# 3-D instance norm: one-pass statistics on VectorE, all normalisation on ScalarE, six buffers with stores four tiles behind the loads

## The chip, the cores and the metric

The kernel runs on one core of a Trainium2 chip. The metric is the device time of one execution in microseconds (us). Before the change it is 1252.36 us, the median of 8 runs that lie between 1251.52 and 1253.71 us. The engines that matter are VectorE (DVE in the profile), ScalarE (ACT), GpSimd (POOL), TensorE (PE), and SyncE (SP), which issues the DMAs here. Sixteen DMA engines carry them out.

## What is computed

```python
def setup_inputs():
    batch, channels, (d, h, w) = 8, 64, (32, 64, 64)
    return {"x": np.random.randn(batch, channels, d, h, w).astype(np.float32), "eps": np.float32(1e-5)}

def reference(x, eps):
    mean = np.mean(x, axis=(2, 3, 4), keepdims=True)
    var = np.var(x, axis=(2, 3, 4), keepdims=True)
    return ((x - mean) / np.sqrt(var + eps)).astype(np.float32)
```

There are 8 x 64 = 512 instances of 32 x 64 x 64 = 131,072 float32 values. Each gets its own mean and variance. The input is 268.44 MB and so is the output. Every value is read once and written once.

## The kernel before

**Tiling.** Each instance is cut into 16 rows of 8,192 values, and 8 instances fill the 128 partitions of a tile (`SPLIT` = 16, `IPT` = 8, `F` = 8,192). That makes 64 tiles of 4,096 KB (4.19 million bytes). Group and tile are the same here, since `KPG` is 1. The buffers of the tiles come from a pool of four (line 45), 32 KB a partition each. A tile is normalised in place and stored from the same buffer.

**One tile.** `issue_load` (line 85) puts the load of one tile on the SP queue. `issue_compute` then does the following.

- VectorE sums each row in one instruction over 8,192 values (line 92). Beside it ScalarE squares the same values and accumulates their sum (line 100). The squares themselves go to a bfloat16 scratch tile that nobody reads.
- TensorE adds up the 16 rows of each instance with one small product (line 108). It multiplies by `ones_t`, a 128x128 block matrix that holds 1/16.
- VectorE and ScalarE work out mean, variance, `std`, `scale` and `bias` on operands of one or two values a partition (lines 117 to 149).
- Three engines normalise the tile: VectorE the first 1,024 columns, ScalarE the next 1,024, GpSimd the other 6,144 (lines 158 to 176, `norm_splits` at line 76).

**Order.** One loop goes over the 64 tiles. Its order on the SP queue is: load of tile g, then store of tile g - 2 (`LAG` = 2, lines 182 to 190). SP works its list off strictly in order. The first three loads go out at once, then the store of tile 0, the load of tile 3, the store of tile 1, and so on by turns. After the loop the last two stores follow. Two kinds of wait stand in this list. A store waits until all three engines have normalised their share of its tile. A load waits until the store that last used its buffer, four tiles back, has landed completely. The scheduler puts in these waits; the order itself is that of the Python loop.

**DMA.** A transfer covers 128 rows of 32,768 bytes. The trace shows each row as one packet, so a transfer has 128 packets, 8 for each of the 16 DMA engines. Each engine reports the end of its own share, so each transfer has sixteen landing events in the trace, and it counts as landed with the last of them. All loads and stores run on one DMA queue, named q1 in the profile. Two more kinds of record, on q14 and q8 with the kind `instruction`, belong to no line of the kernel.

Of the kernel before, what the change touches and what calls it, by code (L numbers as in the profile page):

```python
# [1 line left out]

# [4 lines left out]


@with_exitstack
def kernel(  # L10
    ctx: ExitStack,
    tc: tile.TileContext,
    x: bass.AP,
    eps: bass.AP,
    out: bass.AP,
):
    nc = tc.nc
    fp32 = mybir.dt.float32

    P = 128  # L20
    B, C, D, H, W = x.shape
    n_inst = B * C
    n_elem = D * H * W

    eps_f = float(eps)

    SPLIT = 16
    IPT = P // SPLIT
    F = n_elem // SPLIT

    G = 8
    KPG = G // IPT
    n_groups = n_inst // G

    LAG = 2

    x_packed = x.rearrange("b c d h w -> (b c) (d h w)").rearrange(
        "(k i) (s f) -> k (i s) f", i=IPT, s=SPLIT
    )
    out_packed = out.rearrange("b c d h w -> (b c) (d h w)").rearrange(  # L40
        "(k i) (s f) -> k (i s) f", i=IPT, s=SPLIT
    )

    singles = ctx.enter_context(tc.tile_pool(name="singles", bufs=1))
    data_pool = ctx.enter_context(tc.tile_pool(name="data", bufs=4))
    scratch_pool = ctx.enter_context(tc.tile_pool(name="scratch", bufs=2))
    stat_pool = ctx.enter_context(tc.tile_pool(name="stats", bufs=4))
    psum_pool = ctx.enter_context(tc.tile_pool(name="psum", bufs=4, space=bass.MemoryType.PSUM))

    ones_t = singles.tile([P, P], fp32)  # L50
    nc.vector.memset(ones_t, 1.0 / SPLIT)  # L51
    blk_pattern = [[-SPLIT, P // SPLIT], [0, SPLIT]]
    nc.gpsimd.affine_select(  # L53
        out=ones_t,
        in_=ones_t,
        pattern=blk_pattern,
        compare_op=mybir.AluOpType.is_ge,
        fill=0.0,
        base=0,
        channel_multiplier=1,  # L60
    )
    nc.gpsimd.affine_select(  # L62
        out=ones_t,
        in_=ones_t,
        pattern=[[SPLIT, P // SPLIT], [0, SPLIT]],
        compare_op=mybir.AluOpType.is_ge,
        fill=0.0,
        base=SPLIT - 1,
        channel_multiplier=-1,
    )  # L70

    inv_F = 1.0 / F

    c1 = F // 8
    c2 = F // 4
    norm_splits = [
        (nc.vector, 0, c1),
        (nc.scalar, c1, c2),
        (nc.gpsimd, c2, F),
    ]  # L80

    def issue_load(g):
        x_tiles = data_pool.tile([P, KPG, F], fp32, name="x_tiles")
        src = x_packed[g * KPG : (g + 1) * KPG].rearrange("k p f -> p k f")
        nc.sync.dma_start(out=x_tiles, in_=src)
        return x_tiles

    def issue_compute(g, x_tiles):
        psums = stat_pool.tile([P, KPG, 2], fp32, name="psums")

        for k in range(KPG):
            nc.vector.reduce_sum(  # L92
                out=psums[:, k, 0:1],
                in_=x_tiles[:, k, :],
                axis=mybir.AxisListType.X,
            )
            sq_scratch = scratch_pool.tile(
                [P, F], mybir.dt.bfloat16, name="sq_scratch"
            )
            nc.scalar.activation(  # L100
                out=sq_scratch,
                in_=x_tiles[:, k, :],
                func=mybir.ActivationFunctionType.Square,
                accum_out=psums[:, k, 1:2],
            )

        tot = psum_pool.tile([P, KPG, 2], fp32, name="tot")
        nc.tensor.matmul(  # L108
            out=tot,
            lhsT=ones_t,  # L110
            rhs=psums,
            start=True,
            stop=True,
        )

        me2 = stat_pool.tile([P, KPG, 2], fp32, name="me2")
        nc.vector.tensor_scalar(  # L117
            out=me2,
            in0=tot,
            scalar1=inv_F,  # L120
            scalar2=None,
            op0=mybir.AluOpType.mult,
        )
        mean = me2[:, :, 0]
        e2 = me2[:, :, 1]

        msq = stat_pool.tile([P, KPG], fp32, name="msq")
        nc.vector.tensor_mul(out=msq, in0=mean, in1=mean)  # L128

        var_eps = stat_pool.tile([P, KPG], fp32, name="var_eps")  # L130
        nc.vector.scalar_tensor_tensor(  # L131
            out=var_eps,
            in0=e2,
            scalar=eps_f,
            in1=msq,
            op0=mybir.AluOpType.add,
            op1=mybir.AluOpType.subtract,
        )

        std = stat_pool.tile([P, KPG], fp32, name="std")  # L140
        nc.scalar.activation(  # L141
            out=std,
            in_=var_eps,
            func=mybir.ActivationFunctionType.Sqrt,
        )
        scale = stat_pool.tile([P, KPG], fp32, name="scale")
        nc.vector.reciprocal(out=scale, in_=std)  # L147
        bias = stat_pool.tile([P, KPG], fp32, name="bias")
        nc.vector.scalar_tensor_tensor(  # L149
            out=bias,  # L150
            in0=mean,
            scalar=-1.0,
            in1=scale,
            op0=mybir.AluOpType.mult,
            op1=mybir.AluOpType.mult,
        )

        for k in range(KPG):
            for eng, lo, hi in norm_splits:
                if eng is nc.scalar:  # L160
                    nc.scalar.activation(  # L161
                        out=x_tiles[:, k, lo:hi],
                        in_=x_tiles[:, k, lo:hi],
                        func=mybir.ActivationFunctionType.Identity,
                        scale=scale[:, k : k + 1],
                        bias=bias[:, k : k + 1],
                    )
                else:
                    eng.tensor_scalar(  # L169
                        out=x_tiles[:, k, lo:hi],  # L170
                        in0=x_tiles[:, k, lo:hi],
                        scalar1=scale[:, k : k + 1],
                        scalar2=bias[:, k : k + 1],
                        op0=mybir.AluOpType.mult,
                        op1=mybir.AluOpType.add,
                    )

    def issue_store(g, x_tiles):
        dst = out_packed[g * KPG : (g + 1) * KPG].rearrange("k p f -> p k f")
        nc.sync.dma_start(out=dst, in_=x_tiles)  # L180

    pending = {}
    for g in range(n_groups):
        x_tiles = issue_load(g)
        issue_compute(g, x_tiles)
        pending[g] = x_tiles
        if g >= LAG:
            issue_store(g - LAG, pending.pop(g - LAG))
    for g in range(n_groups - LAG, n_groups):
        issue_store(g, pending.pop(g))  # L190


# [1 line left out]
_INS = ['x', 'eps']  # L194
_OUTS = [((8, 64, 32, 64, 64), 'float32')]
#: Inputs that are plain numbers.
_NUMBERS = {'eps': 9.999999747378752e-06}


# [26 lines left out]
```

## Time and profile before

| what | value |
|---|---|
| median of 8 runs | 1252.36 us (1251.52 to 1253.71) |
| the profiled execution: its own time | 1251.52 us |
| its span, from the first to the last instruction | 1249.7 us |
| data moved, and mean rate | 536.88 MB, 430 GB/s |
| DVE busy | 659.0 us, 53% |
| ACT busy | 550.6 us, 44% |
| POOL busy | 380.5 us, 30% |
| PE busy | 35.8 us, 3% |

The span leaves out 1251.52 - 1249.7 = 1.8 us around the instructions. The profile is a page in six parts: busy times, the span in 40 slices, the DMA queues, the chain of work that ended last, the costliest groups of instructions, and the DMA issues. The trace behind it answers finer questions: busy time and DMA rate in any stretch, who waited for whom on any engine, and the start, length and landing of DMA packets. A group's row reads: line, engine, operation, output and input with their shapes, count; then busy time in all and mean ns of one; then the idle time of the engine just before them and what ended most of it. In the trace the trivial operations on one value a partition (lines 117 to 149) take about 0.16 us each on VectorE and 0.20 us on ScalarE.

### The profile page before, as it was taken

Reading aid. Unit: us, or ns where it says so; the run is one execution under the profiler, and the core shown is the slowest. Engines: PE = TensorE matmul, PEld = TensorE weight load, DVE = VectorE, ACT = ScalarE, POOL = GpSimd, SP = SyncE. Lnnn points to the kernel's source line nnn. Section 1 sums busy time; section 2 is a strip of 40 time slices with the busy share of each in tenths; the row PEclk is TensorE's granted clock in tenths of the full one; section 3 lists DMA queues with packets and bytes.
Section 4 is the critical chain, followed back from the end, with each engine's and each line's share of the span. In section 5 each row is a group of like instructions: output and inputs, shape, how many; then the busy total and the mean of one; then the engine's idle time right before and its main releaser. Section 6 shows DMA issues by size and latency. Waiting matters only on the chain.

```text
span 1249.7 us, 1827 instructions
## 1 busy us (share of the span) xinstructions
PE 35.8 (3%) x128; PEld 32.1 (3%) x128; DVE 659.0 (53%) x449; ACT 550.6 (44%) x258; POOL 380.5 (30%) x70
## 2 busy tenths in 40 slices
PE   0000000000000000000000000000000000000000
PEld 0000000000000000000000000000000000000000
DVE  5746455464554645646546455464563645646543
ACT  5534445354453543534435445354453543534432
POOL 2332332323323233132231332323323233132231
DMA  9999999999999999999999999999999999999998
GB/s 403 420 434 433 428 430 430 432 434 428 433 431 432 436 433 431 430 436 434 436 430 431 432 434 436 433 432 430 434 435 434 431 430 433 434 435 433 433 430 359
DMA packets 18444, 536.99 MB, mean 430 GB/s; under 512 B 2048, under 2 KB 2048, under 8 KB 2048
## 3 DMA queue, kind: packets, MB, share of 16 engines
q1 hardware_dynamic: 18432, 536.88, 99.7%
q14 instruction: 11, 0.09, 0.0%
q8 instruction: 1, 0.02, 0.0%
HBM read 268.44 MB, written 268.44 MB: 430 GB/s over the span
## 4 chain that ended last, share of the span: by engine, by line
DMA 74%; issue 16%; POOL 7%; DVE 1%; POOLq 1%; PE 0%; ACT 0%
DMA out_dram<-x_tiles 39%; DMA x_tiles<-in_x_dram 35%; POOL x_tiles L169 7%; DVE psums L92 1%; POOLq L221 0%; DVE x_tiles L169 0%; POOLq L169 0%; PE tot L108 0%; ACT std L141 0%; DVE scale L147 0%; DVE me L117 0%; DVE bias L149 0%; DVE var_eps L131 0%; DVE msq L128 0%
## 5 line engine op out<-in xcount | busy, mean ns | idle before, releaser
L92 DVE TENSOR_REDUCE psums<-x_tiles 128x1 f32<-128x8192 f32 x64 | 555.9, 8686 | 493.1 <-DMA x_tiles<-in_x_dram 493.1
L100 ACT ACTIVATE sq_scratch<-x_tiles 128x8192 bf16<-128x8192 f32 x64 | 449.9, 7029 | 461.5 <-DMA x_tiles<-in_x_dram 461.5
L169 POOL TENSOR_SCALAR x_tiles<-x_tiles,scale,bias 128x6144 f32<-128x6144 f32 x64 | 379.6, 5931 | 855.2 <-DVE bias L149 633.9
L161 ACT ACTIVATE x_tiles<-x_tiles,bias,scale 128x1024 f32<-128x1024 f32 x64 | 79.4, 1241 | 40.4 <-DVE bias L149 40.4
L141 ACT ACTIVATE std<-var_eps 128x1 f32<-128x1 f32 x64 | 13.0, 203 | 178.7 <-DVE var_eps L131 178.7
L108 PE MATMUL tot<-psums,ones_t 128*128 128x2 f32 x128 | 35.8, 349 | 1193.5 <-DVE psums L92 1193.5
L108 PEld LDWEIGHTS tot<-psums,ones_t 128*128 128x128 f32 x128 | 32.1, 312 | 1197.1 <-issue 1197.1
L169 DVE TENSOR_SCALAR x_tiles<-x_tiles,scale,bias 128x1024 f32<-128x1024 f32 x64 | 52.0, 812 | 2.5 <-DVE bias L149 0.2
L117 DVE TENSOR_SCALAR me<-tot 128x2 f32<-128x2 f32 x64 | 10.2, 159 | 47.6 <-PE tot L108 47.6
L147 DVE RECIPROCAL scale<-std 128x1 f32<-128x1 f32 x64 | 10.5, 163 | 21.8 <-ACT std L141 21.8
L100 ACT ACTIVATION_READ_ACCUMULATOR sq_scratch<-x_tiles 128x1 f32 x64 | 11.9, 186 | 0.0
L128 DVE TENSOR_TENSOR msq<-me 128x1 f32<-128x1 f32 x64 | 10.2, 159 | 2.2
L131 DVE SCALAR_TENSOR_TENSOR var_eps<-me,msq 128x1 f32<-128x1 f32 x64 | 10.2, 159 | 2.2
L149 DVE SCALAR_TENSOR_TENSOR bias<-me,scale 128x1 f32<-128x1 f32 x64 | 10.1, 159 | 2.2
L100 ACT ACT_TABLE_LOAD x1 | 1.3, 1283 | 0.8 <-PEq L207 0.8
L141 ACT ACT_TABLE_LOAD x1 | 1.3, 1283 | 0.0
L51 DVE MEMSET ones_t<- 128x128 f32 x1 | 0.2, 165 | 0.9 <-PEq L207 0.9
L53 POOL TENSOR_SCALAR_AFFINE_SELECT ones_t<-ones_t 128x128 f32<-128x128 f32 x1 | 0.3, 343 | 0.6 <-DVE ones_t L51 0.6
L62 POOL TENSOR_SCALAR_AFFINE_SELECT ones_t<-ones_t 128x128 f32<-128x128 f32 x1 | 0.3, 338 | 0.1
L207 POOL MEMSET const-float32-0.0<- 128x1 f32 x1 | 0.1, 100 | 0.3 <-issue 0.3
L207 POOL MEMSET const-bfloat16-1.0<- 128x1 bf16 x1 | 0.1, 103 | 0.0
L207 POOL MEMSET const-uint8-127<- 128x1 uint8 x1 | 0.1, 103 | 0.0
(1 smaller groups left out, 0.1 us busy)
## 6 DMA issues: line engine op xcount, KB each, us to landing
x_tiles<-in_x_dram SPq DMA_DIRECT2D x64, 4096.0 KB, 29.0
out_dram<-x_tiles SPq DMA_DIRECT2D x64, 4096.0 KB, 31.5
```

The source lines that it names most:

```text
L92: nc.vector.reduce_sum(out=psums[:, k, 0:1], in_=x_tiles[:, k, :], axis=mybir.AxisListType.X,)
L100: nc.scalar.activation(out=sq_scratch, in_=x_tiles[:, k, :], func=mybir.ActivationFunctionType.Square, accum_out=psums[:, k, 1:2],)
L108: nc.tensor.matmul(out=tot, lhsT=ones_t, rhs=psums, start=True, stop=True,)
L117: nc.vector.tensor_scalar(out=me2, in0=tot, scalar1=inv_F, scalar2=None, op0=mybir.AluOpType.mult,)
L128: nc.vector.tensor_mul(out=msq, in0=mean, in1=mean)
L131: nc.vector.scalar_tensor_tensor(out=var_eps, in0=e2, scalar=eps_f, in1=msq, op0=mybir.AluOpType.add, op1=mybir.AluOpType.subtract,)
L141: nc.scalar.activation(out=std, in_=var_eps, func=mybir.ActivationFunctionType.Sqrt,)
L147: nc.vector.reciprocal(out=scale, in_=std)
L149: nc.vector.scalar_tensor_tensor(out=bias, in0=mean, scalar=-1.0, in1=scale, op0=mybir.AluOpType.mult, op1=mybir.AluOpType.mult,)
L161: nc.scalar.activation(out=x_tiles[:, k, lo:hi], in_=x_tiles[:, k, lo:hi], func=mybir.ActivationFunctionType.Identity, scale=scale[:, k : ...
L169: eng.tensor_scalar(out=x_tiles[:, k, lo:hi], in0=x_tiles[:, k, lo:hi], scalar1=scale[:, k : k + 1], scalar2=bias[:, k : k + 1], op0=mybir ...
L207: nc = _bacc.Bacc("TRN2", target_bir_lowering=False, num_devices=1)
```

## The change

- **Statistics.** The row sum and the squares go. VectorE takes 16 `bn_stats` over 512 values each and one `bn_aggr`, which together give each row's mean and variance. Two small products with the same block matrix (now `avg`) average the means and then the variances, the latter with the squared distance of the row's mean added. The scratch tile goes.
- **Normalisation.** One ScalarE instruction over all 8,192 columns, in place of three on three engines. GpSimd has no work in the loop any more.
- **Order.** Six buffers in place of four. The store of tile g - 4 follows the load of tile g. The first five loads go out at once, and the last four stores stand behind the loop. A load waits for the store six tiles back. A store waits for ScalarE alone.

The diff, cut to its core:

```diff
-    data_pool = ctx.enter_context(tc.tile_pool(name="data", bufs=4))
-    scratch_pool = ctx.enter_context(tc.tile_pool(name="scratch", bufs=2))
+    SLOTS = 6
+    FMAX = nc.vector.BN_STATS_FMAX
+    n_chunks = F // FMAX
+    data_pool = ctx.enter_context(tc.tile_pool(name="data", bufs=SLOTS))
...
-            nc.vector.reduce_sum(out=psums[:, k, 0:1], in_=x_tiles[:, k, :], axis=mybir.AxisListType.X)
-            nc.scalar.activation(out=sq_scratch, in_=x_tiles[:, k, :],
-                func=mybir.ActivationFunctionType.Square, accum_out=psums[:, k, 1:2])
+        for c in range(n_chunks):
+            nc.vector.bn_stats(out=st[:, c, :], in_=t[:, c * FMAX : (c + 1) * FMAX])
+        nc.vector.bn_aggr(out=mv, in_=st)
...
-        nc.tensor.matmul(out=tot, lhsT=ones_t, rhs=psums, start=True, stop=True)
+        nc.tensor.matmul(out=mean_ps, lhsT=avg, rhs=mv[:, 0:1], start=True, stop=True)
+        nc.vector.tensor_sub(out=dist, in0=mv[:, 0:1], in1=mean_ps)
+        nc.vector.scalar_tensor_tensor(out=part, in0=dist, scalar=dist, in1=mv[:, 1:2], op0=Alu.mult, op1=Alu.add)
+        nc.tensor.matmul(out=var_ps, lhsT=avg, rhs=part, start=True, stop=True)
+        nc.vector.tensor_scalar(out=var, in0=var_ps, scalar1=eps_f, scalar2=None, op0=Alu.add)
...
-            for eng, lo, hi in norm_splits:
-                if eng is nc.scalar:
-                    nc.scalar.activation(out=x_tiles[:, k, lo:hi], in_=x_tiles[:, k, lo:hi], ...)
-                else:
-                    eng.tensor_scalar(out=x_tiles[:, k, lo:hi], in0=x_tiles[:, k, lo:hi], ...)
+        nc.scalar.activation(out=t, in_=t, func=Act.Identity, scale=scale, bias=bias)
...
-    LAG = 2
+    LAG = 4
+    for g in range(n_tiles):
+        t = load(g)
+        scale, bias = coefficients(statistics(t))
+        normalise(t, scale, bias)
+        held[g] = t
+        if g >= LAG:
+            store(g - LAG, held.pop(g - LAG))
+    for g in range(n_tiles - LAG, n_tiles):
+        store(g, held.pop(g))
```

Counted over all instructions of the built programs, waits and the closing ones among them, VectorE goes from 577 to 1,417 instructions, ScalarE from 386 to 262, GpSimd from 210 to 22, SP from 271 to 204, and TensorE from 136 to 137. The number, size and shape of the loads and stores stay as they were.

More of the change, by code (lines that the diff above doesn't have):

```diff
@@ L4 @@
 import concourse.tile as tile
-from concourse import bass_utils, mybir
+from concourse import mybir
 from concourse._compat import with_exitstack
@@ L18 @@
     fp32 = mybir.dt.float32
+    Alu = mybir.AluOpType
+    Act = mybir.ActivationFunctionType
     P = 128
@@ L29 @@
     F = n_elem // SPLIT
-    G = 8
-    KPG = G // IPT
-    n_groups = n_inst // G
-    LAG = 2
-    x_packed = x.rearrange("b c d h w -> (b c) (d h w)").rearrange(
+    n_tiles = n_inst // IPT
+    SLOTS = 6
+    FMAX = nc.vector.BN_STATS_FMAX
+    n_chunks = F // FMAX
+    x_t = x.rearrange("b c d h w -> (b c) (d h w)").rearrange(
         "(k i) (s f) -> k (i s) f", i=IPT, s=SPLIT
     )
-    out_packed = out.rearrange("b c d h w -> (b c) (d h w)").rearrange(
+    out_t = out.rearrange("b c d h w -> (b c) (d h w)").rearrange(
         "(k i) (s f) -> k (i s) f", i=IPT, s=SPLIT
@@ L44 @@
     singles = ctx.enter_context(tc.tile_pool(name="singles", bufs=1))
-    data_pool = ctx.enter_context(tc.tile_pool(name="data", bufs=4))
-    scratch_pool = ctx.enter_context(tc.tile_pool(name="scratch", bufs=2))
[L47 to L52, printed above, removed]
+    data_pool = ctx.enter_context(tc.tile_pool(name="data", bufs=SLOTS))
+    stat_pool = ctx.enter_context(tc.tile_pool(name="stats", bufs=3))
+    psum_pool = ctx.enter_context(
+        tc.tile_pool(name="psum", bufs=2, space=bass.MemoryType.PSUM)
+    )
+    avg = singles.tile([P, P], fp32, name="avg")
+    nc.vector.memset(avg, 1.0 / SPLIT)
     nc.gpsimd.affine_select(
[L54 to L57, printed above, removed]
+        out=avg,
+        in_=avg,
+        pattern=[[-SPLIT, IPT], [0, SPLIT]],
+        compare_op=Alu.is_ge,
         fill=0.0,
@@ L62 @@
     nc.gpsimd.affine_select(
[L63 to L66, printed above, removed]
+        out=avg,
+        in_=avg,
+        pattern=[[SPLIT, IPT], [0, SPLIT]],
+        compare_op=Alu.is_ge,
         fill=0.0,
@@ L70 @@
     )
[L72 to L113, printed above, removed]
-        )
-        me2 = stat_pool.tile([P, KPG, 2], fp32, name="me2")
@@ new lines, in load, with statistics @@
+    def load(g):
+        t = data_pool.tile([P, F], fp32, name="xt")
+        nc.sync.dma_start(out=t, in_=x_t[g])
+        return t
+    def statistics(t):
+        st = stat_pool.tile([P, n_chunks, nc.vector.BN_STATS_DIM], fp32, name="st")
+        for c in range(n_chunks):
+            nc.vector.bn_stats(out=st[:, c, :], in_=t[:, c * FMAX : (c + 1) * FMAX])
+        mv = stat_pool.tile([P, nc.vector.BN_AGGR_DIM], fp32, name="mv")
+        nc.vector.bn_aggr(out=mv, in_=st)
+        return mv
@@ new lines, in coefficients @@
+    def coefficients(mv):
+        mean_ps = psum_pool.tile([P, 1], fp32, name="mean_ps")
+        nc.tensor.matmul(out=mean_ps, lhsT=avg, rhs=mv[:, 0:1], start=True, stop=True)
+        dist = stat_pool.tile([P, 1], fp32, name="dist")
+        nc.vector.tensor_sub(out=dist, in0=mv[:, 0:1], in1=mean_ps)
+        part = stat_pool.tile([P, 1], fp32, name="part")
+        nc.vector.scalar_tensor_tensor(
+            out=part,
+            in0=dist,
+            scalar=dist,
+            in1=mv[:, 1:2],
+            op0=Alu.mult,
+            op1=Alu.add,
+        )
+        var_ps = psum_pool.tile([P, 1], fp32, name="var_ps")
+        nc.tensor.matmul(out=var_ps, lhsT=avg, rhs=part, start=True, stop=True)
+        var = stat_pool.tile([P, 1], fp32, name="var")
@@ L117, in issue_compute @@
         nc.vector.tensor_scalar(
[L118 to L122, printed above, removed]
-        )
[L124 to L146, printed above, removed]
+            out=var, in0=var_ps, scalar1=eps_f, scalar2=None, op0=Alu.add
+        )
+        std = stat_pool.tile([P, 1], fp32, name="std")
+        nc.scalar.activation(out=std, in_=var, func=Act.Sqrt)
+        scale = stat_pool.tile([P, 1], fp32, name="scale")
@@ L147, in issue_compute @@
         nc.vector.reciprocal(out=scale, in_=std)
-        bias = stat_pool.tile([P, KPG], fp32, name="bias")
+        bias = stat_pool.tile([P, 1], fp32, name="bias")
         nc.vector.scalar_tensor_tensor(
             out=bias,
-            in0=mean,
+            in0=mean_ps,
             scalar=-1.0,
             in1=scale,
-            op0=mybir.AluOpType.mult,
-            op1=mybir.AluOpType.mult,
-        )
-        for k in range(KPG):
-            for eng, lo, hi in norm_splits:
-                if eng is nc.scalar:
[L161 to L167, printed above, removed]
-                else:
[L169 to L186, printed above, removed]
+            op0=Alu.mult,
+            op1=Alu.mult,
+        )
+        return scale, bias
+    def normalise(t, scale, bias):
+        nc.scalar.activation(out=t, in_=t, func=Act.Identity, scale=scale, bias=bias)
@@ L187, with store @@
+    def store(g, t):
+        nc.sync.dma_start(out=out_t[g], in_=t)
+    LAG = 4
+    held = {}
+    for g in range(n_tiles):
[3 more added lines that the diff above has]
+        held[g] = t
         if g >= LAG:
-            issue_store(g - LAG, pending.pop(g - LAG))
-    for g in range(n_groups - LAG, n_groups):
-        issue_store(g, pending.pop(g))
+            store(g - LAG, held.pop(g - LAG))
+    for g in range(n_tiles - LAG, n_tiles):
+        store(g, held.pop(g))
```

## The prediction

> **What bounds the kernel now.** I read the page's top first, then its DMA lines.
>
> ```profile
> span 1249.7 us, 1827 instructions
> PE 35.8 (3%) x128; PEld 32.1 (3%) x128; DVE 659.0 (53%) x449; ACT 550.6 (44%) x258; POOL 380.5 (30%) x70
> ...
> GB/s 403 420 434 433 428 430 430 432 434 428 433 431 432 436 433 431 430 436 434 436 430 431 432 434 436 433 432 430 434 435 434 431 430 433 434 435 433 433 430 359
> ...
> q1 hardware_dynamic: 18432, 536.88, 99.7%
> q14 instruction: 11, 0.09, 0.0%
> ```
>
> No compute engine is busy more than 53% of the time. The 16 DMA engines are busy 99.7% with the loads and stores, so they are the bound. The rate dips only in the first two slices and the last. The change leaves the bytes alone, so only three things can move the end: idle time of the DMA engines, longer packets, and other work on them.
>
> The last slice looks like idle time to be won. The stretches there (us; busy time of PE, PEld, DVE, ACT, POOL; clock; DMA share; GB/s) and SP's own waits say more:
>
> ```profile
> 1232.00:1233.00 1.00, 0.00 (x0) 0.00 (x0) 0.00 (x0) 0.00 (x0) 1.00 (x1) 1.00 0.76 328
> 1233.00:1234.00 1.00, 0.00 (x0) 0.00 (x0) 0.00 (x0) 0.00 (x0) 1.00 (x1) 1.00 0.61 262
> 1234.00:1235.00 1.00, 0.00 (x0) 0.00 (x0) 0.00 (x0) 0.00 (x0) 1.00 (x1) 1.00 0.38 164
> 1235.00:1236.00 1.00, 0.00 (x0) 0.00 (x0) 0.00 (x0) 0.00 (x0) 1.00 (x1) 1.00 0.30 131
> 1236.00:1237.00 1.00, 0.00 (x0) 0.00 (x0) 0.00 (x0) 0.00 (x0) 0.73 (x1) 1.00 0.30 131
> ...
> SPq L221 <- DMA out_dram<-x_tiles: 11.5, 2, 9.6
> ```
>
> The last store was issued at 1236.8, when GpSimd had finished the last tile. Before that up to 70% of the DMA engines were out of work. But not all of them: the store before it landed at 1239.2 and the last one 9.6 us later (the second wait), which is one transfer's own time. So the last DMA engine to finish went from store to store without a gap.
>
> Each transfer has 16 landing events, one per DMA engine. From one full landing to the next the median step is 9.686 us. I set each event against a line of such steps from the first event, at 12.56 us. After the first load the 16 shares lie within 0.5 us of each other. Before the last store they lie from 0.5 to 6.3 us behind the line. Each engine has a lateness of its own, and **the latest of the sixteen sets the end**: 12.56 + 127 x 9.6855 + 6.23 = 1248.9, then 0.8 us of closing.
>
> **Where the lateness is from.** Two causes show in the packet records. A packet of 32,768 bytes takes 1.213 us at the median. In the first 400 us, packets at the end of a load, where engines change over to a store, often take 1.3 to 2.1 us. That stops as the engines drift apart. The other cause is the `instruction` records of q14. Four of them, of 8,192 bytes, begin when VectorE has started 67, 193, 319 and 445 instructions: one per 126. 8,192 bytes over 126 to 128 instructions is 64 bytes each, so I read them as VectorE's program being fetched. Around the last three, one landing series jumps:
>
> ```
> VectorE instructions before it   fetch at, us   lateness of one DMA engine, before -> after, us
> 193                              420.55         3.97 -> 4.94
> 319                              691.27         4.72 -> 5.69
> 445                              962.00         5.53 -> 6.45
> ```
>
> In between, that series only drifts down slowly (4.94 to 4.72, 5.69 to 5.53). The series fit together as one engine, and it is the one that ends last. A fetch costs it 0.92 to 0.97 us: 0.31 for itself, the rest in a slowed packet (1.76 to 1.79 us). The first fetch, at 146.50, falls among the changeovers and can't be separated.
>
> **The change, part by part.**
>
> *VectorE's program.* This is what I charge. The built program has 1,417 VectorE instructions, before 577, because 16 `bn_stats` a tile replace one sum. Fetches at 65 + 128 k with k from 0 up to 1,417 are 11, before 4. Seven more at 0.95 us are **+6.65 us** on the engine that already ends last. Nothing hides them: that engine is never idle, and the next load waits for the latest share. Bounds: nothing, if the fetches find another engine or an idle spot; 7 x 0.97 = 6.8 at the top, and 3 us more if this engine draws as much changeover lateness as the worst engine did. That one reached 5.4 with no such jump; this one has 6.3 - 4 x 0.95 = 2.5 without its fetches. ScalarE, GpSimd and SP fetch less, on engines that weren't last: nothing.
>
> The Trainium skill, "Runtime: NRT & Kernel Launch", section "Instruction fetch mechanics", speaks against this charge: refills come in 16 KiB blocks of 256 instructions, and a crossing is mostly hidden. The trace has 8,192 bytes per 126 instructions and the three jumps above. By the page's rule the sum would stay at 1251.5; by the rows it is 1258.2, and I go by the rows.
>
> *VectorE's time.* There is no `bn_stats` row. The rows on both sides are the sum over 8,192 values (8,686 ns) and the trivial operations (159 ns). A pass over 512 of the same values is at least 8,686/16 = 543 ns and about 159 + 512 x 1.04 = 692 ns with an own start; two passes would be 1.24 us. I take 692, since the count per pass is the sum row's. A tile is then 16 x 0.69 + 16 gaps of 0.035 = 11.6 us. `bn_aggr`, four small operations, two waits for TensorE (0.74 each) and the root (about 0.5) add 3.5: 15 us. A tile's turn on the DMA engines is 2 x 9.686 = 19.4 us, so the transfers hide it. The cover ends at (19.4 - 3.5)/16 = 0.99 us per `bn_stats`.
>
> *ScalarE.* Normalising 8,192 columns lies between the square's 7.03 us, of the same size, and 8 x 1.24 = 9.9 us, from the 1,024-column row. I take 7.0. The next tile's root waits behind it, but comes 19 us later. Hidden. GpSimd's 5.9 us and the squares go from work that was hidden too: nothing.
>
> *Order on SP.* A load still waits for the store issued two turns earlier (six back against four, stores four behind against two), so when it goes out, one load and one store, 19.4 us, lie ahead of it, as now. The new first store waits for 13 + 15 + 7 to 10 = 35 to 38 us, while five loads keep the DMA engines busy until about 51. All later loads stand behind that store, and it is early enough. Before, DMA share was 1.00 in every stretch of 80 us from 80 to 1200, so there was nothing to win in the loop. At the end, four stores (38.7 us) cover the last tile's 15 + 10 = 25 us. That fills the hole at 1232 to 1237 for the early engines, which don't set the end: nothing. Bounds: -3.6 us, the mean idle time of the 16 engines there, if the late one gains after all; nothing lost while these covers hold.
>
> *Sum.* On the profiled execution: 1251.5 + 6.65 = 1258.2. The eight runs have their median 0.8 above it; I don't add that, since a late engine may meet fewer changeovers. **Prediction: 1258.2 us**, 0.5% slower.
>
> **Rivals.**
>
> 1. *The fetches don't show.* They fall on engines with room, or the three jumps were chance. For it: they are 0.09 MB. Against it: three jumps of one size on one series. Then nothing is left: about 1252, from 1251 to 1254.
> 2. *Faster: the hole at the end is real.* Six buffers fill it and all engines run on. This mechanism gives 2.7 us (the shares missing from 1232 to 1237) to 3.6 us: 1248 to 1249. It decides if the latest engine is ahead of 1236.8 when the last store goes out; before, it was 2.4 us behind it.
> 3. *VectorE becomes the bound.* Past 0.99 us per `bn_stats` the loop runs at VectorE's pace. At 1.24 us a tile is 20.4 + 3.5 = 23.9 us, and 64 of them about 1,530 us. Against it: the sum's row reads one value per 1.04 ns.
>
> **How the numbers follow.** A run of this kernel can be told from no change at about 0.2%, or 2.5 us: below 1249.9 is faster, above 1254.9 slower. The forecast has 0.70, with 1255 to 1261 as its own range (6.65 with up to 3 us more or less of changeover lateness). Rival 1 has 0.15, rival 2 has 0.09, rival 3 has 0.06. Slower: most of 0.70 and all of 0.06, 0.75. Same: 0.16. Faster: 0.09. Forecast and rival 1 together hold 0.85, so the range is 1251 to 1261.
>
> **What would show it.** Right: q1 still near 99.7%, about 16 records of q14 (11 now, 7 more for VectorE, a few less for the shorter programs), 11 of them in steps of about 110 us; one landing series that steps up 0.95 us at each and ends about 12 to 13 us behind the line; slices before the last still at 430 or a little less. Wrong: the same records and no steps (rival 1); the latest series back at 3 us or below (rival 2); VectorE busy near 100% and loads that wait for it (rival 3). The forecast fails as a whole if the sixteen latenesses aren't bound to engines.

## The result and the profile after

The changed kernel takes 1261.4 us, the median of 11 executions (1257.0 to 1267.3), against 1252.1 us for the kernel before on the same chips. The ratio is 1.0073, with a 95% interval of 1.0060 to 1.0085. So the change costs 0.7%. The forecast said slower, for the cause that the runs below show, but its 1258.2 us and its range up to 1261 were too low. The profiled execution took 1258.55 us, 1256.5 of it the span.

The page of the changed kernel, its head and its DMA lines:

```profile
span 1256.5 us, 2417 instructions
PE 75.1 (6%) x256; PEld 64.2 (5%) x256; DVE 705.8 (56%) x1409; ACT 476.0 (38%) x129; POOL 0.9 (0%) x6
...
GB/s 401 423 431 431 432 433 431 433 431 434 432 433 433 433 433 432 434 433 434 432 434 432 433 431 433 433 431 434 434 431 433 434 434 433 434 434 433 434 433 260
...
q1 hardware_dynamic: 18432, 536.88, 99.2%
q14 instruction: 14, 0.11, 0.0%
q8 instruction: 2, 0.03, 0.0%
```

No compute engine came near 100%. Until the last slice the rate is that of before, 433 GB/s. All that was lost shows in one place: 260 GB/s in the last slice, where 359 stood. DVE has three times as many instructions as before. The q14 records rose from 11 to 14, although GpSimd, ScalarE and SP have shorter programs.

The groups that were priced without a row (line, engine, operation, shapes, count; busy, mean ns; idle time before and what ended it):

```profile
L80 DVE BATCH_NORM_STATS2 st<-xt 128x6 f32<-128x512 f32 x1024 | 613.8, 678 | 399.0 <-DMA xt<-in_x_dram 399.0
L122 ACT ACTIVATE xt<-xt,bias,scale 128x8192 f32<-128x8192 f32 x64 | 461.7, 7213 | 27.1 <-DVE bias L111 27.1
```

A `bn_stats` takes 678 ns and a whole tile's normalisation 7.2 us. Both are hidden: VectorE still waits 399 us in all for loads.

The end of the span, in stretches of 3 us (us; busy time of PE, PEld, DVE, ACT, POOL; clock; DMA share; GB/s):

```profile
1233.00:1236.00 3.00, 0.00 (x0) 0.00 (x0) 0.00 (x0) 0.00 (x0) 0.00 (x0) 1.00 1.06 459
1236.00:1239.00 3.00, 0.00 (x0) 0.00 (x0) 0.00 (x0) 0.00 (x0) 0.00 (x0) 1.00 0.91 393
1239.00:1242.00 3.00, 0.00 (x0) 0.00 (x0) 0.00 (x0) 0.00 (x0) 0.00 (x0) 1.00 1.09 470
1242.00:1245.00 3.00, 0.00 (x0) 0.00 (x0) 0.00 (x0) 0.00 (x0) 0.00 (x0) 1.00 0.38 164
1245.00:1248.00 3.00, 0.00 (x0) 0.00 (x0) 0.00 (x0) 0.00 (x0) 0.00 (x0) 1.00 0.13 55
1248.00:1251.00 3.00, 0.00 (x0) 0.00 (x0) 0.00 (x0) 0.00 (x0) 0.00 (x0) 1.00 0.08 33
1251.00:1254.00 3.00, 0.00 (x0) 0.00 (x0) 0.00 (x0) 0.00 (x0) 0.00 (x0) 1.00 0.05 22
```

This is the picture to remember. All compute is over. One DMA engine of sixteen is a share of 0.06, and from 1248 on the share is 0.05 to 0.08: a single engine still stores its part of the last tile, while fifteen have nothing to do. The hole at 1232 to 1237 of before is filled (1.06 and 0.91 in the first two stretches), as planned, and it gained nothing.

The sixteen landing events of the last store say the same. Their lateness is set against steps of 9.6855 us from the first event of the first load, as in the prediction:

```
            first series   second latest   latest   last landing at, us
before      5.08           5.40            6.23     1248.85
changed     0.35           4.84            13.18    1255.67
```

Fifteen engines finish earlier than before. The sixteenth is 7 us later, and it sets the end: 1255.67 - 1248.85 = 6.8 us, the whole difference of the two spans. Its lateness grows in steps, and the steps fall at fetches of 8,192 bytes that come with every 120 to 132 VectorE instructions. From the second to the last they are 0.96, 0.78, 0.79, 0.81, 0.79, 0.96, 0.81, 0.80, 0.79 and 0.82 us, 8.3 in all. (The fetch at 919 us has a neighbour at 912 us that falls on none of these counts, so it is for another engine; the latest series takes no step there.)

### The profile page after: what moved, and what is told of

Read it like the earlier page. It is cut to its first block, busy times and chain, and to the rows that moved or that the text cites. A ratio compares the mean times of both kernels' runs of the same rounds, so it can differ in the third digit from the quotient of the medians.

```text
span 1256.5 us, 2417 instructions
## 1 busy us (share of the span) xinstructions
PE 75.1 (6%) x256; PEld 64.2 (5%) x256; DVE 705.8 (56%) x1409; ACT 476.0 (38%) x129; POOL 0.9 (0%) x6
## 3 DMA queue, kind: packets, MB, share of 16 engines
q1 hardware_dynamic: 18432, 536.88, 99.2%
## 4 chain that ended last, share of the span: by engine, by line
DMA 92%; DVE 3%; ACT 1%; SPq 1%; issue 0%; PE 0%; ACTq 0%
DMA out_dram<-xt 89%; DMA xt<-in_x_dram 3%; DVE st L80 2%; ACT xt L122 1%; SPq L74 1%; PE var_ps L101 0%; DVE mv L82 0%; PE mean_ps L88 0%; DVE part L92 0%; ACT std L107 0%; DVE scale L109 0%; DVE var L103 0%; DVE dist L90 0%; DVE bias L111 0%; ACTq L107 0%
## 5 line engine op out<-in xcount | busy, mean ns | idle before, releaser
L80 DVE BATCH_NORM_STATS2 st<-xt 128x6 f32<-128x512 f32 x1024 | 613.8, 678 | 399.0 <-DMA xt<-in_x_dram 399.0
L122 ACT ACTIVATE xt<-xt,bias,scale 128x8192 f32<-128x8192 f32 x64 | 461.7, 7213 | 27.1 <-DVE bias L111 27.1
L107 ACT ACTIVATE std<-var 128x1 f32<-128x1 f32 x64 | 13.0, 203 | 723.6 <-DVE var L103 723.6
L88 PE MATMUL mean_ps<-mv,avg 128*128 128x1 f32 x128 | 37.6, 363 | 1112.1 <-DVE mv L82 1112.1
L88 PEld LDWEIGHTS mean_ps<-mv,avg 128*128 128x128 f32 x128 | 32.2, 313 | 1117.5 <-DVE mv L82 1094.1
L101 PE MATMUL var_ps<-part,avg 128*128 128x1 f32 x128 | 37.5, 362 | 32.1 <-DVE part L92 32.1
L82 DVE BATCH_NORM_AGGREGATE mv<-st 128x2 f32<-128x96 f32 x64 | 37.6, 588 | 2.2
L103 DVE TENSOR_SCALAR var<-var_ps 128x1 f32<-128x1 f32 x64 | 10.1, 158 | 43.3 <-PE var_ps L101 43.3
L101 PEld LDWEIGHTS var_ps<-part,avg 128*128 128x128 f32 x128 | 32.0, 310 | 37.6 <-DVE part L92 37.6
L92 DVE SCALAR_TENSOR_TENSOR part<-dist,mv 128x1 f32<-128x1 f32 x64 | 14.1, 220 | 2.3
```

What stands on the lines that cost most here:

```text
L80: nc.vector.bn_stats(out=st[:, c, :], in_=t[:, c * FMAX : (c + 1) * FMAX])
L82: nc.vector.bn_aggr(out=mv, in_=st)
L88: nc.tensor.matmul(out=mean_ps, lhsT=avg, rhs=mv[:, 0:1], start=True, stop=True)
L92: nc.vector.scalar_tensor_tensor(out=part, in0=dist, scalar=dist, in1=mv[:, 1:2], op0=Alu.mult, op1=Alu.add,)
L101: nc.tensor.matmul(out=var_ps, lhsT=avg, rhs=part, start=True, stop=True)
L103: nc.vector.tensor_scalar(out=var, in0=var_ps, scalar1=eps_f, scalar2=None, op0=Alu.add)
```

## The experiments

**Theory.** VectorE's longer program is fetched over the one DMA engine that ends last, and each fetch makes it later. **Rivals.** Six buffers and stores four behind slow the DMA engines (order); or `bn_stats` and ScalarE's whole tiles slow the packets (access). Each time below is a median beside the kernel before on the same chip, with the ratio's interval. "Latest" is the lateness of the latest series in the trace.

### The changed kernel with few VectorE instructions

```diff
-        for c in range(n_chunks):
-            nc.vector.bn_stats(out=st[:, c, :], in_=t[:, c * FMAX : (c + 1) * FMAX])
-        nc.vector.bn_aggr(out=mv, in_=st)
+        nc.vector.reduce_sum(out=sums[:, 0:1], in_=t, axis=mybir.AxisListType.X)
+        nc.scalar.activation(out=sq, in_=t, func=Act.Square, accum_out=sums[:, 1:2], saturate=False)
```

`sq` is a scratch tile of one-byte values, and the coefficients are worked out as in the kernel before.

> The changed kernel's order, six buffers and ScalarE normalisation, but VectorE takes one row sum a tile and ScalarE the squares: 393 VectorE instructions in place of 1,417. Theory: 3 fetches in place of 11, 8 x 0.85 to 0.95 us less, latest series 5 to 6 us behind the line, 1250 to 1253 us. Rival (six buffers and stores four behind cost the DMA engines time): stays at 1258 to 1262. Rival (ScalarE writing whole tiles in place slows the packets): stays too.

Measured: 1252.5 us, ratio 1.0006 (0.9997 to 1.0014). Order and in-place ScalarE are both here, and the loss is gone. Both fall as causes. Its page has half the fetches of the changed kernel's:

```profile
q14 instruction: 7, 0.06, 0.0%
```

Its latest series ends at 7.35, a little more than expected, and for another reason than expected. Only three fetches are VectorE's, and at the second and third, at 597 and 1012 us, this series takes no step. So another DMA engine ends last here, and its lateness is from slowed packets at the ends of loads: 7.1 us by 407 us. This run takes `bn_stats` away together with the instructions, so it doesn't tell these two apart; the copies below do.

### The kernel before with a longer VectorE program

```diff
+        for _ in range(13):
+            nc.vector.memset(pad_t, 0.0)
```

> The kernel before with 13 memsets of one column a tile added on VectorE, which nobody reads: 1,409 VectorE instructions, nothing else changed. Theory: 11 fetches, 7 x 0.95 = 6.6 us more, 1258 to 1262 us. Both rivals (order; whole tiles on ScalarE or bn_stats reading SBUF): 1252, since none of that is here; the memsets are 13 x 0.1 us of a tile's 19.4.

Measured: 1266.0 us, ratio 1.0113 (1.0100 to 1.0127). This run does not decide. The scheduler did not leave the memsets with their tiles: VectorE had started 842 instructions by 192 us, where the kernel without the padding had started 77 by 175 us. Between 190 and 240 us the earliest of the sixteen series falls from 1.9 to 12.6 us behind the line and stays there, so this delay held up all of them alike. The latest still steps by 0.94 to 0.99 us at single fetches, but the time can't be put down to those. The padding was made to stay with its tile:

```diff
+        for _ in range(13):
+            nc.vector.tensor_copy(out=pad_t, in_=bias)
```

> The kernel before with 13 one-column copies a tile on VectorE that read this tile's bias, so that they stay with their tile: 1,409 VectorE instructions, nothing else changed. Theory: 11 fetches evenly over the run, each about 0.8 us on the latest landing series, 7 x 0.8 = 5.6 us more and 1 to 4 us of slowed packets at changeovers beside it: 1257 to 1263 us. Rivals (order, in-place ScalarE, bn_stats): 1252.

Measured: 1257.9 us, ratio 1.0047 (1.0035 to 1.0059). Its page:

```profile
span 1256.9 us, 2659 instructions
...
q14 instruction: 18, 0.15, 0.0%
...
L180 DVE COPY pad_t<-bias 128x1 f32<-128x1 f32 x832 | 127.5, 153 | 26.5
```

The 832 copies read four bytes a partition each and take 153 ns. Nothing else differs from the kernel before, and the time rises by 6.1 us. The q14 records are 7 more, which is the number predicted for VectorE's own. The latest series takes nine clear steps of 0.88 to 0.96 us between 285 and 1210 us and ends 13.6 us behind the line; the next is at 5.9 before the last store. That is the theory, shown with no part of the change in it. It is 6.1 of the 9.3 us that the change costs between the medians; which part of the change brings the other 3 us is not separated.

### The order alone

```diff
-    data_pool = ctx.enter_context(tc.tile_pool(name="data", bufs=4))
+    data_pool = ctx.enter_context(tc.tile_pool(name="data", bufs=6))
...
-    LAG = 2
+    LAG = 4
```

> The kernel before with six buffers and stores four behind, everything else kept (the squares' scratch is one tile of one-byte values, so that it fits). Theory: VectorE has 575 instructions as before, so 1251 to 1253 us, and the idle hole before the last store is filled without gain. Rival (order): 1258 to 1262. Rival (the hole at the end is worth something): 1248 to 1249.

Measured: 1252.5 us, ratio 1.0004 (0.9995 to 1.0012). The stretches where the hole was, and the end:

```profile
1232.00:1235.00 3.00, 0.00 (x0) 0.00 (x0) 0.00 (x0) 0.00 (x0) 0.00 (x0) 1.00 0.96 415
1235.00:1237.00 2.00, 0.00 (x0) 0.00 (x0) 0.00 (x0) 0.00 (x0) 0.00 (x0) 1.00 1.02 442
...
1246.00:1249.30 3.30, 0.00 (x0) 0.00 (x0) 0.00 (x0) 0.00 (x0) 0.00 (x0) 1.00 0.09 40
```

The share at 1235 to 1237 is 1.02, where it was 0.30. Yet the span is 1249.3 us, 0.4 less than before, and the ratio holds no gain. The early engines now stop earlier; the latest ends where it ended. Rival 2 of the prediction falls here, and so does the rival that the order costs time.

### The statistics alone

`bn_stats`, `bn_aggr` and the two products of the change replace lines 89 to 138 of the kernel before. Four buffers, `LAG` = 2 and the three-engine normalisation stay.

> The kernel before with the one-pass statistics alone: four buffers, stores two behind, normalisation on three engines as before; 1,601 VectorE instructions. Theory: 12 to 13 fetches, 1258 to 1264 us, as slow as the whole change or a little slower. Rivals (order; in-place ScalarE): 1252.

Measured: 1273.8 us, ratio 1.0163 (1.0140 to 1.0186), more than the whole change. SP's list in its first 50 us (start, length, instruction):

```profile
0.80 1.33 SPq L85 DMA_DIRECT2D x_tiles<-in_x_dram  x3
32.00 0.35 SPq L157 DMA_DIRECT2D out_dram<-x_tiles  x1
32.38 0.43 SPq L85 DMA_DIRECT2D x_tiles<-in_x_dram  x1
45.51 0.34 SPq L157 DMA_DIRECT2D out_dram<-x_tiles  x1
```

The first store goes out at 32.0 us, where it went out at 29.9 before. Three loads last until about 32, so the DMA engines run dry: the first series is 1.80 us late at that store, against 0.49 before. In the change two more loads are in flight then. The traced execution is one of 1267.9 us, so 5.9 us of the median have no trace. In it the latest series ends 22.6 us behind the line, against 13.2 in the changed kernel's first profile. Of these 9.4 us, the trace has about 1.7 at the start, 2.3 at VectorE's fetches (12 against 11, and mostly 0.95 us each), 3.3 at ends of loads after 830 us, and 1.2 at the end: the last store went out at 1254.1 us, when the store before it had all but landed (1254.3), so here all sixteen engines ran out of work. After 400 us, 83 packets are slowed (over 1.26 us), against 14. So beside the new statistics the rest of the change (buffers, order and ScalarE's normalisation, not told apart here) is worth some 12 us between the medians, though the order alone is worth nothing.

### A longer program still, and another engine's

The changed kernel with the same 13 copies a tile on VectorE, 2,249 instructions in all:

> The changed kernel with the same 13 copies a tile on VectorE: 2,249 instructions in place of 1,417. Theory: 6 or 7 fetches more, latest series 18 to 24 us behind the line, 1266 to 1272 us. If the fetches are not the cause: 1257 to 1262, as the changed kernel.

Measured: 1273.3 us (1267.2 to 1281.0), ratio 1.0178 (1.0151 to 1.0205). In its trace, of an execution of 1278.3 us, the latest series ends at 32.9, far past what was expected. Up to 690 us it grows mostly at the fetches, to 12.4 us behind the line after ten of them. By 803 us it is 15.5 us behind after twelve, and 1.2 us of that came at ends of loads. By 903 us it is 17.7 us behind the earliest series. From there on the earliest falls back as fast as the latest, as I read it because buffers come free only with the latest engine's share, and the rate of the whole core sinks:

```profile
600.00:800.00 200.00, 11.71 (x40) 10.00 (x40) 131.31 (x357) 77.55 (x21) 0.00 (x0) 1.00 1.00 433
...
900.00:1000.00 100.00, 5.86 (x20) 5.01 (x20) 65.16 (x175) 35.85 (x11) 0.00 (x0) 1.00 1.00 416
1000.00:1100.00 100.00, 5.87 (x20) 5.01 (x20) 65.15 (x175) 36.42 (x11) 0.00 (x0) 1.00 1.00 415
```

The DMA share stays at 1.00 while the rate falls from 433 to 415: the packets themselves are longer. There are 481 slowed packets after 400 us. The other fifteen series end together, 15.1 to 17.5 us behind the line.

The kernel before with the 13 copies on GpSimd (`nc.gpsimd.tensor_copy`), 1,042 GpSimd instructions:

> The same padding on GpSimd instead: 1,042 GpSimd instructions, VectorE 637. Theory: 8 fetches for GpSimd in place of 2, on another DMA engine's series; that one starts from 1 to 5 us and gains 6 x 0.5 to 0.9 us, so the latest ends 6 to 10 us behind the line: 1252 to 1257. If any fetch for any engine hits the one latest series: 1257 to 1259. If fetches cost nothing: 1252.

Measured: 1253.4 us, ratio 1.0011 (1.0002 to 1.0019). The latest series now steps by 0.63 or 0.64 us when GpSimd has started 572, 700, 828 and 956 instructions, 128 apart, and ends at 9.8. It takes none at VectorE's fetches, at 321 and 451 VectorE instructions. So another engine's program costs a DMA engine time too, in another series and a smaller step. The median rises by only 1.7 us; the trace is of the longest of the 11 executions, 1254.85 us.

### Fewer changeovers

The row-sum kernel and the changed kernel, each with two loads and then two stores on SP's list:

```diff
+    for g in range(0, n_tiles, 2):
+        pair = [load(g), load(g + 1)]
...
+        if g >= LAG:
+            store(g - LAG, held.pop(g - LAG))
+            store(g + 1 - LAG, held.pop(g + 1 - LAG))
```

> The row-sum kernel (393 VectorE instructions) with the SP list in pairs: two loads, then two stores, so that the engines change over from load to store half as often. Theory (two parts of lateness, program fetches and changeovers): the changeovers' 3 to 5 us fall by about half, latest series 3 to 5 us behind the line, 1249 to 1251 us. If changeovers cost nothing, or their cost is per run and not per changeover: 1252 to 1253, as the row sums alone.

Measured: 1253.1 us, ratio 1.0010 (1.0001 to 1.0019). The theory's gain did not come. There were more slowed packets, not fewer (199 against 111), and the early series end at 2.5 where they ended at 0.4. When a load goes out, only one transfer is ahead of it. That the engines therefore wait for the latest and start again together is my reading; no run shows it by itself.

> The changed kernel with the SP list in pairs, all else as in the change. When a load goes out, only one transfer, 9.7 us, is ahead of it, against two. Theory: the 11 fetches cost their 9 us as before; once the latest engine is more than about 9 us behind, the others run out of work, wait for it and bunch up, and then meet more slowed packets at changeovers: 1260 to 1270, and the other series end 4 to 10 us behind the line together. If waiting for the latest engine does no harm: 1256 to 1260.

Measured: 1259.8 us, ratio 1.0063 (1.0050 to 1.0075), at the edge between both expectations. The other series do bunch, 8.1 to 10.9 us behind the line, and 285 packets after 400 us are slowed. The latest series ends at 14.7, which is within what the changed kernel itself shows. So waiting for the latest engine slows packets, and here it cost the end little.

### The changed kernel again, for its spread

> The changed kernel once more, for its spread and a second trace. Every theory: 1257 to 1267 us, median about 1261. Theory (VectorE's program is fetched over the DMA engine that ends last): again 11 fetches of 8,192 bytes, and the latest landing series 12 to 18 us behind the line, by how far the time of the traced execution lies above 1258. Rival (order): the lateness grows at loads and stores, not at fetches.

> The changed kernel once more, one look, for what makes one execution longer than another. Theory: fetches add the same 9 us each time; the rest, slowed packets on the latest engine late in the run, makes the difference between 1257 and 1267 us. Rival: a fetch costs more in a long execution.

> The changed kernel in another single look, for the same question. Theory: again about 9 us of fetches, and slowed packets on the latest engine for whatever the execution takes above 1257. Rival: a fetch costs more in a long execution.

Measured: in a new group of runs 1260.5 us (1257.0 to 1269.0), ratio 1.0076 (1.0051 to 1.0101); two single executions took 1258.5 and 1263.5. With the first profile there are four traces of one program:

```
execution, us   latest, us   ten fetch steps from 129 us on, us   further steps after 900 us, us
1258.55         13.2         8.3                                  0
1258.54         13.2         8.3                                  0
1260.88         15.5         8.3                                  1.9
1263.46         18.0         8.3                                  4.1
```

The fetch steps are the same in every execution. What differs is the last column: in the longer two, the latest engine loses 0.14 to 0.85 us at a time at ends of loads, once it is about 11.5 us behind the line or more. The end of the longest:

```profile
1251.00:1254.00 3.00, 0.00 (x0) 0.00 (x0) 0.00 (x0) 0.00 (x0) 0.00 (x0) 1.00 0.05 22
1254.00:1257.00 3.00, 0.00 (x0) 0.00 (x0) 0.00 (x0) 0.00 (x0) 0.00 (x0) 1.00 0.08 33
1257.00:1261.40 4.40, 0.00 (x0) 0.00 (x0) 0.00 (x0) 0.00 (x0) 0.00 (x0) 1.00 0.03 15
```

One engine alone for 11.4 us. Two of the four passed 12 us without those losses, so what decides it is open. Distance alone does not: the kernel before with the copies ends 13.6 us behind the line, has no such loss in its trace, and its five executions lie within 1.6 us. Losses by an engine that is 11 us or more behind the earliest stand only in traces of kernels with `bn_stats`, and the kernel before with the copies is the only one without it that gets so far. That the reads of `bn_stats` have a part in these losses is a rival that no run rules out. An execution as long as 1267 us has no trace.

## Why the prediction was right or wrong

- **The bound and the end: right.** The time is the latest DMA engine's. The hole of before was worth nothing (order alone: 1.0004).
- **VectorE's fetches: right in kind and number, a little large in size.** 11 fetches were predicted and 11 came. Ten of them cost 0.83 us on average in place of 0.95. Padding alone, with nothing of the change, gave +6.1 us for 7 more records. In the form that the charge names, seven more: 5.8 us in place of 6.65. A detail of the charge doesn't add up: the record's 0.31 us and a packet of 1.76 to 1.79 in place of 1.21 us make 0.86 to 0.89, not 0.92 to 0.97; the rest of the step has no row.
- **Runtime rule: the rows held.** By the Trainium skill's "Runtime: NRT & Kernel Launch", "Instruction fetch mechanics", a crossing is mostly hidden. It is hidden from VectorE as far as the profile shows: every wait of VectorE in its list has another cause. It isn't hidden from the loads and stores on the same DMA engine: 0.83 us each. The trace again has 8,192 bytes per 120 to 132 instructions, where the page has 16 KiB per 256.
- **The term that failed: this engine's share of changeover lateness.** The prediction took 2.5 us from the trace of before, left it unchanged in the sum, and allowed up to 3 us more in the range. Without fetches (11 x 0.83 = 9.1), the four traces of the changed kernel have 4.1, 4.1, 6.4 and 8.9 us. Part of it is early and in all four: by 470 us, without four fetches, the series has 5.0 to 5.3 us, where the same series of before has 3.0 by 410 us (3.97 less one fetch). The other part is late and in two of four: 1.9 and 4.1 us at ends of loads after 900 us, where the latest series of before has none. Whether the fetches bring this about, by putting the engine far behind, or the new statistics do, stays open.
- **And the sum.** It was made on one profiled execution, which it met (1258.2 against 1258.55), and then given as the median. The meeting is partly luck, since two misses nearly cancel there: the fetches cost 0.85 us less, and the changeovers some 1.1 us more (13.18 - 6.23 - 5.8). The kernel before varies by 2 us in its first 8 runs, and the 0.8 us from its profiled execution to its median were left out by choice; with them the sum is 1259.0. The changed kernel varies by 10 us, mostly upwards, and its median lies 2.8 us above the profiled execution. So 1261.4 lies just past the range.
- **VectorE, ScalarE, order in the start and end: right.** It took 678 ns against 692 taken; 7.2 us against 7.0; the first store at 33.2 us against 35 to 38, with five loads in flight. None of it shows in the time. One thing was not said: with the new statistics three loads ahead are too few, since the DMA engines then run dry at 32 us. For the hole, the lines shown give 2.7 us of idle time; the 3.6 that stands beside it as the idle time has no line, and nothing rests on it, since the hole gained nothing.
- **What would show it: mostly.** The steps of 0.8 to 0.96 us and 13 us behind the line came as written. The q14 records are 14 and not about 16, and q1 is at 99.2%, a little under the 99.7 that was named.

## What to carry to other kernels

When the DMA engines are busy 99% of the time and every transfer is split over all of them, the slowest one sets the end: look at the spread of a transfer's landing events and at the DMA share of the last microseconds, not at the mean. On such a kernel, instructions have a price even on an idle engine, because their fetch runs over one of the same DMA engines: here 0.8 to 0.96 us per 128 VectorE instructions. The price shows in the time where that DMA engine is the one that ends last; with few VectorE instructions, another engine ended last and the price was gone. Replacing one long instruction by sixteen short ones can lose, although every one of them is hidden.

## What the runs showed of the hardware that was not expected

- Within an execution, the fetches for one compute engine met one landing series: ten steps of 0.77 to 0.96 us for VectorE in each of four executions, alike to 0.03 us. GpSimd's came in another series, at 0.63 to 0.64 us. That a series is one DMA engine is read from its continuity; the records don't name the engine.
- With a latest engine far enough behind, packets got longer on the others too. With the longest program the rate fell from 433 to 415 GB/s at a DMA share of 1.00, and 481 packets after 400 us were slowed, against 14 in the changed kernel's first profile.
- The changed kernel's executions spread over 1257 to 1269 us, those of the kernel before over 1250 to 1255. Distance of the latest engine is not enough for that: with the copies added to the kernel before, the latest ends 13.6 us behind, and five executions lie between 1257.1 and 1258.7 us.
